# Short blocks merged ahead of the long sequence's last gate columns, output products by weight unit, late attention outputs split in place

## The chip, the cores and the metric

One core of one Trainium2 chip. The metric is the device time of the whole kernel in microseconds (us), as the median of several runs. Before the change it is 2817.07 us (three runs, 2802.38 to 2821.04).

## The reference

An encoder layer over two sequences (1 x 1024 and 1 x 2048 tokens, "short" and "long" here), with 16 meta tokens ahead of each, 1024 channels and shared weights. Cut to what matters:

```python
xn = rmsnorm(h, g_pre)
proj = xn @ w_in + b_in                        # 1024 -> 6672 columns
ya = (neighbourhood_attention(na_q, na_k, na_v, rpb) * silu(na_z)) @ w_a
yb = (mlstm(ml_qk, ml_v, ml_g, ml_o, ...) * silu(ml_z)) @ w_b
ga, gb = split(sigmoid(mg))                    # two gate vectors of 1024
y = (ga * ya + gb * yb) @ w_out
return h + rmsnorm(y, g_post)                  # the meta tokens are dropped
```

Attention has 8 heads of 64 over a window of 8 x 16 grid places; the mLSTM has 4 heads of 128 and runs in both directions in chunks.

## The kernel before

All products are made in fp32r with operands split in a rounded high and a low part, three matmuls each (high by high, low by high, high by low; lines 170 to 172 for the helper mm3). PE's instructions stand in the order in which the program writes them; those of the other engines are ordered by a scheduler at build time, each engine then taking its own in that fixed order. DMAs of these stages are issued from SP's queue, in order.

Two streams of work are interleaved on PE. The *dense* stream is written out in PLAN (line 44): projection columns per half sequence ("akqzt", "Gh" and so on: a = mLSTM q and k, k, q, z = attention, t = values and others token by token, G and h = gate columns), the first column groups of the short sequence by a seven-product scheme ("S"), and the items ("f", s, b), one for each block of 512 tokens: two for the short sequence (s = 0), four for the long one (s = 1). The *sparse* stream is the mLSTM and the attention of both sequences (STEPS, line 45): mLSTM short, attention short, mLSTM long, attention long; after each of its steps dense work of a set cost is put in. Dense work is what fills PE while the sparse steps wait for ACT and DVE.

An f item (final, line 1802) has two parts. The *merges*: for each of 8 channel tiles ft, four k steps of the mLSTM output (br = 1) and four of the attention output (br = 0) against w_b and w_a, each result times its gate (L1841), added (L1843), split in mh (ACT, L1844) and mlo (DVE, L1845). The inputs yh and yl of a block are loaded by yload (line 1763): it loads a finished output from DRAM into yl (L1774), rounds it into yh on ACT (L1793 is where the profile puts it) and subtracts on DVE (L1778). The attention's last step (na_out, line 1246) adds the two halves of a head (L1259, L1261), multiplies by the gate z (L1263) and writes the block's output to DRAM (L1264). The *output products* against w_out: four column blocks cq of 256 columns, each of two weight units (a = 0, 1: 512 input channels each), times four token tiles tt of 128. For a column block, both units are taken; each token tile has 8 k steps of three matmuls (L1875 to L1877) into a PSUM tile of its own, of three ("pj"); then ACT squares it into a sum (sqj, L1905) and DVE multiplies by g_post into yo (L1906). final_out normalises and adds the residual xres (L1956), and writes out (L1957). The last item makes column blocks 2 and 3 together, tile by tile, and closes each tile as soon as it is complete.

Weights come in units of 512 KB (wpump): the first time raw, rounded on ACT (L269), its low part on DVE (L270), and both stored (L285); later both parts are loaded (L262). Four buffers each (NBW) hold whi and wlo; a unit's buffer is given back by wdone, which starts the next load. g_post is held whole in one tile ("gain"), scaled once by -0.125 (L1859).

Of the kernel before, what the change touches and what calls it, by code (L numbers as in the profile page):

```python
# [18 lines left out]
P = 128  # L19
# [24 lines left out]
PLAN = ((0, 0, "akt"),) + FIRST + ((1, 0, "at"), (1, 1024, "akqzt"), (1, 0, "kqzGh"), (1, 1024, "Gh"), ("f", 0, 0), ("f", 0, 1), ("f", 1, 0), ("f", 1, 1), ("f", 1, 2), ("f", 1, 3))  # L44
# [81 lines left out]
class K:  # L126
# [3 lines left out]
    def __init__(self, tc, ins, outs):  # L130
        self.tc, self.nc = tc, tc.nc
        self.xs = []
        self.i, self.o = ins, outs
        self.wreq, self.wraw, self.wrdy, self.wout = deque(), deque(), deque(), 0
        self.wseen, self.wkept, self.xkept = set(), {}, {}
        self.rwait = {}
        self.xput, self.turn, self.last, self.turns = deque(), 0, None, False
        self.need, self.gpost = False, None
# [53 lines left out]
    def gain(self, name):  # L192

        g = self.wp.tile([P, D], F32, name="gain", bufs=1)
        self.nc.sync.dma_start(g, _bc(self.i[name], 0, D))
        return g
# [1049 lines left out]
    def na_out(self, np_, unit, s):  # L1246
# [15 lines left out]
        if hh and cb == 3:  # L1262
            nc.vector.tensor_tensor(yg, yg, zt, op=ALU.mult)  # L1263
            nc.sync.dma_start(self.YA[s][rt][pr][:, :], yg)  # L1264
# [294 lines left out]
    def ml_outputs(self, mp, s, h, g, NB, sts, norms):  # L1559
# [23 lines left out]
        def split(b):  # L1583
            if b < NB:
                raw = raws.pop(b)
                if s and b % 3 == 2 and self.gpost is None:
# [176 lines left out]
    def yload(self, s, b):  # L1763
# [17 lines left out]
        late, half = [4, 5, 6, 7, 0, 1, 2, 3], None  # L1781
        while todo or late or half is not None:
# [19 lines left out]
    def final(self, s, b, nxt):  # L1802
# [21 lines left out]
        for ft, br in [(0, 1)] + [x for f in range(KT) for x in ((f + 1, 1), (f, 0)) if x[0] < KT]:  # L1824
# [3 lines left out]
            for k in range(4 * br, 4 * br + 4):  # L1828
                self.need = True
                while k not in self.yk:  # L1830
                    if next(self.ygen) == "wait" and k not in self.yk:
                        yield True
# [24 lines left out]
        if self.fresh:  # L1857
            self.fresh = False
            nc.vector.tensor_scalar(self.gpost, self.gpost, -0.125, None, op0=ALU.mult)  # L1859
# [10 lines left out]
        def prods(p, tt, ws, k0, k1):  # L1870
            o = p[:, :256]
            xs = slice(tt * P, tt * P + P)
            for k in range(k0, k1):
                wh, wl = ws[k // 4][0][:, k % 4, :], ws[k // 4][1][:, k % 4, :]
                nc.tensor.matmul(o, mh[:, k, xs], wh, start=k == 0, stop=False)  # L1875
                nc.tensor.matmul(o, mh[:, k, xs], wl, start=False, stop=False)  # L1876
                nc.tensor.matmul(o, ml[:, k, xs], wh, start=False, stop=k == KT - 1)  # L1877

        for cqs in (((0,), (1,), (2,), (3,)) if nxt else ((0,), (1,), (2, 3))):
            wq = [self.wtake(2) for _ in cqs]  # L1880
            first = {}
            if cqs[0] == 0:
                for tt in range(2):
                    first[tt] = self.psum("pj", [P, 512])
                    prods(first[tt], tt, wq[0], 0, 7)
                    yield 21 * C256
            turns = [(tt, x) for tt in range(4) for x in zip(cqs, wq)]
            if len(cqs) > 1:
                turns[1:3] = turns[2], turns[1]
            for tt, (cq, ws) in turns:  # L1890
                if tt in first:
                    p = first[tt]
                    prods(p, tt, ws, 7, 8)
                else:
                    p = self.psum("pj", [P, 512])
                    prods(p, tt, ws, 0, 4)
                    if tt == 3:
                        self.wdone()
                    yield 12 * C256
                    prods(p, tt, ws, 4, 8)  # L1900
                if tt == 3:
                    self.wdone()
                o = p[:, :256]
                dst = yt[tt][:, cq * 256:(cq + 1) * 256]
                nc.scalar.activation(sqj, o, AF.Square, accum_out=ssq[:, tt, cq:cq + 1])  # L1905
                nc.vector.tensor_tensor(dst, o, self.gpost[:, cq * 256:(cq + 1) * 256], op=ALU.mult)  # L1906
                if cq == 3 and not nxt:
                    for _ in self.final_out(s, t0, yt, ssq, tt, tt + 1):
                        pass
                if nxt and hook is None:  # L1910
                    if nxt[0] != "f":
                        nres = []
                        hook = self.build_half(*nxt[:2], nres)
                    else:
                        hook = self.ystart(*nxt[1:])
                if hook:
                    next(hook, None)
                yield (3 if tt in first else 12) * C256
# [10 lines left out]
    def final_out(self, s, t0, yt, ssq, a, b):  # L1929
# [17 lines left out]
        r = self.rsqrt8(fp, sv[:, a:b], [P, b - a])  # L1947
        yield
# [14 lines left out]
    def dense(self, ctx):  # L1963
# [11 lines left out]
        for j, item in enumerate(PLAN):  # L1975
# [6 lines left out]
            if s == "f":  # L1982
                if self.gpost is None:
                    self.gpost = self.gain("g_post")
                    self.fresh = True
# [111 lines left out]
```

## Time and profile before

| | |
|---|---|
| three runs, median (lowest, highest) | 2817.07 us (2802.38, 2821.04) |
| the profiled execution, its own time | 2810.6 us |
| its span | 2808.8 us |
| mean granted TensorE clock | 0.989 |
| PE busy | 2728.9 us (97%) |
| DVE, ACT busy | 1729.2 us (62%), 1501.9 us (53%) |
| DMA | 666.47 MB, 237 GB/s |

"Busy" is the time in which an engine has an instruction running; matmuls are pipelined, so two neighbours overlap, and a matmul of 256 columns lasts 0.28 us in the rows but follows the one before it after 0.12. In rows of time, the columns are the start in us, the duration in us, the engine, the line, the operation, what is written and read, the shapes, and in brackets how long the engine stood idle before and who ended that. PEld is the load of the stationary operand. SPq is an issue of a DMA. In rows of stretches there are the busy time of each engine with its instructions, the granted TensorE clock (1.00 is full), the mean busy share of the 16 DMA engines, and GB/s.

From 1470 to 2060 us the mLSTM of the long sequence runs beside projection columns; from 2060 to 2690 its attention beside the first five f items; then the last item stands alone.

### The profile page before, as it was taken

How to read it: one execution, taken by the hardware profiler on the slowest of the kernel's cores; microseconds unless marked ns; L12 is line 12 of the kernel's file. 1: busy time of each engine (PE TensorE's matmuls, PEld its weight loads, DVE VectorE, ACT ScalarE, POOL GpSimd, SP SyncE). 2: the span in 40 equal slices, each digit the busy share in tenths (PEclk: the TensorE clock that was granted, in tenths of full speed). 3: DMA queues.
4: the chain of work that ended last, by engine and by line, in shares of the span. 5: the costliest groups of instructions: out<-in, count | busy, mean ns of one | idle time of the engine just before them, and what ended most of it. 6: DMA issues, size and time to landing. Idle time of an engine off the chain costs nothing.

```text
span 2808.8 us, 47866 instructions
## 1 busy us (share of the span) xinstructions
PE 2728.9 (97%) x16840; PEld 2427.4 (86%) x16840; DVE 1729.2 (62%) x4339; ACT 1501.9 (53%) x3348; POOL 124.4 (4%) x298
## 2 busy tenths in 40 slices
PE   8999999999999999999999999999999999999988
PEld 7899988879998778999977888888888898988978
DVE  5534664534667636566624767665667868787754
ACT  5222454433446646655534666565657676777731
POOL 0220000005000000320000000000000000000000
PEclk9999999999999999999999999999999999999989
DMA  9876753396656976756586566885599989898964
GB/s 370 327 252 216 241 181 105 104 349 203 189 171 200 328 232 203 224 178 212 189 286 208 196 208 203 275 280 172 171 314 327 292 268 302 247 323 281 275 216 174
DMA packets 354676, 666.47 MB, mean 237 GB/s; under 512 B 53796, under 2 KB 159220, under 8 KB 354436
## 3 DMA queue, kind: packets, MB, share of 16 engines
q1 hardware_dynamic: 347172, 654.37, 70.4%
q0 software_dynamic: 7264, 9.04, 1.2%
q8 instruction: 133, 2.18, 0.3%
q14 instruction: 107, 0.88, 0.1%
HBM read 446.24 MB, written 216.97 MB: 236 GB/s over the span
## 4 chain that ended last, share of the span: by engine, by line
PE 75%; DMA 14%; DVE 6%; ACT 3%; issue 1%; SPq 1%; DVEq 0%; ACTq 0%; POOLq 0%; POOL 0%
PE pj L170 11%; PE pj L171 11%; PE pj L172 11%; PE pj L619 6%; PE pj L621 6%; PE pj L620 6%; PE pj L1876 3%; PE pj L1875 3%; PE pj L1877 3%; PE sm L1254 2%; PE sm L172 2%; PE tr L1240 2%; PE sm L171 2%; PE sm L170 2%; DMA qk<-cpl 1%; DMA wlo<-wl 1%
## 5 line engine op out<-in xcount | busy, mean ns | idle before, releaser
L170 PE MATMUL pj<-xh,whi 128*128 128x512 f32 (+1 forms) x1480 | 581.7, 393 | 9.8 <-ACT st L544 7.8
L171 PE MATMUL pj<-xl,whi 128*128 128x512 f32 (+1 forms) x1480 | 567.9, 384 | 0.1
L172 PE MATMUL pj<-xh,wlo 128*128 128x512 f32 (+1 forms) x1480 | 566.6, 383 | 0.3 <-DVE wlo L270 0.3
L619 PE MATMUL pj<-whi,xh 128*128 128x256 f32 (+1 forms) x1536 | 438.8, 286 | 2.1 <-DVE stT L634 2.1
L620 PE MATMUL pj<-wlo,xh 128*128 128x256 f32 (+1 forms) x1536 | 432.5, 282 | 0.0
L621 PE MATMUL pj<-whi,xl 128*128 128x256 f32 (+1 forms) x1536 | 432.4, 282 | 0.0
L170 PEld LDWEIGHTS pj<-xh,whi 128*128 128x128 f32 x1480 | 280.2, 189 | 60.5 <-ACT st L544 8.6
L172 PEld LDWEIGHTS pj<-xh,wlo 128*128 128x128 f32 x1480 | 279.8, 189 | 58.0 <-DVE wlo L270 0.5
L171 PEld LDWEIGHTS pj<-xl,whi 128*128 128x128 f32 x1480 | 280.4, 189 | 46.5 <-issue 0.5
L619 PEld LDWEIGHTS pj<-whi,xh 128*128 128x128 f32 x1536 | 289.6, 189 | 2.7 <-DVE stT L634 2.3
L620 PEld LDWEIGHTS pj<-wlo,xh 128*128 128x128 f32 x1536 | 289.4, 188 | 0.2
L621 PEld LDWEIGHTS pj<-whi,xl 128*128 128x128 f32 x1536 | 289.3, 188 | 0.0
L1875 PE MATMUL pj<-whi,mh 128*128 128x256 f32 x768 | 222.1, 289 | 6.5 <-ACT whi L269 3.7
L1876 PE MATMUL pj<-wlo,mh 128*128 128x256 f32 x768 | 218.9, 285 | 3.8 <-DMA wlo<-wl 2.1
L1877 PE MATMUL pj<-whi,mlo 128*128 128x256 f32 x768 | 218.4, 284 | 0.0
L170 PE MATMUL pj<-yh,whi 128*128 128x512 f32 x384 | 156.6, 408 | 9.7 <-ACT yh L1793 9.7
L1875 PEld LDWEIGHTS pj<-whi,mh 128*128 128x128 f32 x768 | 147.5, 192 | 8.3 <-ACT whi L269 4.1
L171 PE MATMUL pj<-yl,whi 128*128 128x512 f32 x384 | 153.2, 399 | 1.3 <-DVE yl L1778 1.3
L172 PE MATMUL pj<-yh,wlo 128*128 128x512 f32 x384 | 152.7, 398 | 0.0
L1876 PEld LDWEIGHTS pj<-wlo,mh 128*128 128x128 f32 x768 | 147.5, 192 | 5.7 <-DMA wlo<-wl 2.6
L1877 PEld LDWEIGHTS pj<-whi,mlo 128*128 128x128 f32 x768 | 147.4, 192 | 0.0
L1243 DVE TENSOR_TENSOR pts<-tr,pts 96x384 fp32r<-96x384 f32 (+2 forms) x192 | 118.6, 618 | 46.7 <-ACT pts L1242 45.8
(378 smaller groups left out, 5643.8 us busy)
## 6 DMA issues: line engine op xcount, KB each, us to landing
whi<-wh SPq DMA_DIRECT2D x152, 512.0 KB
wlo<-wl SPq DMA_DIRECT2D x152, 512.0 KB
wraw<-wu SPq DMA_DIRECT2D x64, 512.0 KB
wh<-whi SPq DMA_DIRECT2D x64, 512.0 KB
wl<-wlo SPq DMA_DIRECT2D x64, 512.0 KB
gt<-st SPq DMA_DIRECT2D x96, 256.0 KB
tg<-gt SPq DMA_DIRECT2D x96, 256.0 KB
xt<-xt SPq DMA_DIRECT2D x32, 512.0 KB
```

Source lines behind the costliest of these rows:

```text
L170: mm(out, ah, bh, start=start, stop=False, **more)
L171: mm(out, ah, bl, start=False, stop=False, **more)
L172: mm(out, al, bh, start=False, stop=stop, **more)
L619: nc.tensor.matmul(o, xh, wh, start=k == 0, stop=False)
L620: nc.tensor.matmul(o, xh, wl, start=False, stop=False)
L621: nc.tensor.matmul(o, xl, wh, start=False, stop=k == KT - 1)
L1240: nc.tensor.transpose(pt[:ks, ch, :], pr_[:, ch * ks:(ch + 1) * ks], self.ident)
L1243: nc.vector.tensor_tensor(pts[:ks, :nb, 1, :], pt[:ks, :nb], pts[:ks, :nb, 0, :].bitcast(F32), op=ALU.subtract)
L1254: nc.tensor.matmul(av[:, cb % 2], vt[:ks, kc // 8 + ch].rearrange("p a b -> p (a b)"), pts[:ks, ch].rearrange("p a b -> p (a b)"), start=c ...
L1875: nc.tensor.matmul(o, mh[:, k, xs], wh, start=k == 0, stop=False)
L1876: nc.tensor.matmul(o, mh[:, k, xs], wl, start=False, stop=False)
L1877: nc.tensor.matmul(o, ml[:, k, xs], wh, start=False, stop=k == KT - 1)
```

## The change

- PLAN: the two items of the short sequence go ahead of (1, 1024, "Gh"), the gate columns of the long sequence's second half. The short merges so run beside the last mLSTM heads, and those gate columns beside attention.
- Output products: a weight unit is taken, used for all four token tiles, and given back, before the next is taken. The four half-done sums of a column block stand in two PSUM tiles, two token tiles in each. The last item's column blocks 2 and 3 keep a PSUM tile for each sum, in another order of tiles.
- g_post is loaded by column block into two small tiles (gp); the factor -0.125 moves to the row factors r (one small DVE operation more in each final_out). The mLSTM's third split buffer, which used the big tile until then, stays in use.
- na_out: when the merges' loader of that block has already begun and has not loaded this output, ACT and DVE split yg straight into yh and yl, without DRAM. This is so for 5 of the 24 outputs.
- The last item's merges take the third mLSTM product ahead of the first attention product.

```diff
-PLAN = (..., (1, 0, "kqzGh"), (1, 1024, "Gh"), ("f", 0, 0), ("f", 0, 1), ("f", 1, 0), ...)
+PLAN = (..., (1, 0, "kqzGh"), ("f", 0, 0), ("f", 0, 1), (1, 1024, "Gh"), ("f", 1, 0), ...)
...
-            nc.sync.dma_start(self.YA[s][rt][pr][:, :], yg)
+            if self.y and self.y[0] == (s, rt) and pr in self.ylate:
+                _, yh, yl = self.y
+                nc.scalar.activation(yh[:, pr], yg, AF.Copy)
+                nc.vector.tensor_tensor(yl[:, pr], yg, yh[:, pr].bitcast(F32), op=ALU.subtract)
+                self.ylate.remove(pr)
+                self.yk.add(pr)
+            else:
+                nc.sync.dma_start(self.YA[s][rt][pr][:, :], yg)
...
+        if not nxt:
+            order[2:4] = order[3], order[2]
...
+        def prods(o, tt, w, a, fresh):
             xs = slice(tt * P, tt * P + P)
+            for k in range(4):
+                f, q = 4 * a + k, w[0][:, k, :]
+                nc.tensor.matmul(o, mh[:, f, xs], q, start=fresh and f == 0, stop=False, skip_group_check=True)
+                nc.tensor.matmul(o, mh[:, f, xs], w[1][:, k, :], start=False, stop=False, skip_group_check=True)
+                nc.tensor.matmul(o, ml[:, f, xs], q, start=False, stop=f == KT - 1, skip_group_check=True)
+
+        def leave(o, tt, cq, gp):
+            nc.scalar.activation(sqj, o, AF.Square, accum_out=ssq[:, tt, cq:cq + 1])
+            nc.vector.tensor_tensor(yt[tt][:, cq * 256:(cq + 1) * 256], o, gp, op=ALU.mult)
+
+        gps = [self.gain(0), self.gain(1)]
+        for cq in range(4 if nxt else 2):
+            banks = [self.psum("pj", [P, 2, 256]) for _ in range(2)]
+            for a in range(2):
+                w = self.wtake(1)[0]
+                for tt in range(4):
+                    o = banks[tt // 2][:, tt % 2]
+                    prods(o, tt, w, a, tt % 2 == 0)
+                    if tt == 3:
+                        self.wdone()
+                    if a:
+                        leave(o, tt, cq, gps[cq])
...
+                    yield 12 * C256
+            if cq < 2:
+                gps.append(self.gain(cq + 2))
+        if not nxt:
+            ws = [[self.wtake(1)[0] for _ in range(2)] for _ in range(2)]
+            turns = [(0, 2), (1, 2)] + [x for tt in range(2, 4) for x in ((tt - 2, 3), (tt, 2))] + [(2, 3), (3, 3)]
+            for tt, cq in turns:
+                o = self.psum("pj", [P, 512])[:, :256]
...
+        nc.vector.tensor_scalar(r, r, -0.125, None, op0=ALU.mult)
```

How the instructions stand, at three places. First PE in the output products of the long sequence's third block, third column block, between two token tiles; the names in brackets are the engines that the row waits for (PE, DVE, Activation = ACT). Before:

```order
L1875 MATMUL pj<-whi,mh 128x256
L1876 MATMUL pj<-wlo,mh 128x256
L1877 MATMUL pj<-whi,mlo 128x256
L1240 MATMUL tr<-ident,prb 104x128 [waits PE_49]
L1240 MATMUL tr<-ident,prb 104x128 x2
L1254 MATMUL sm<-pts,vt 128x256 [waits DVE_49,Activation_49]
L1254 MATMUL sm<-pts,vt 128x256 x3
L1875 MATMUL pj<-whi,mh 128x256
L1876 MATMUL pj<-wlo,mh 128x256
L1877 MATMUL pj<-whi,mlo 128x256
```

And now, between the first and the second token tile of the second weight unit (the new lines 1882 to 1884 are the old 1875 to 1877):

```order
L1882 MATMUL pj<-whi,mh 128x256
L1883 MATMUL pj<-wlo,mh 128x256
L1884 MATMUL pj<-whi,mlo 128x256
L1254 MATMUL sm<-pts,vt 128x256 [waits DVE_49]
L1254 MATMUL sm<-pts,vt 128x256 x2
L1215 MATMUL sm<-kd,stk 128x312
L1216 MATMUL sm<-kx_24012,qB_24010 128x312
L1882 MATMUL pj<-whi,mh 128x256 [waits DVE_49]
L1883 MATMUL pj<-wlo,mh 128x256
L1884 MATMUL pj<-whi,mlo 128x256
```

The first matmul of the next token tile waits for DVE now; by the count of the semaphore, for the gain product (new line 1888) of the tile just done, which reads the other half of the same PSUM tile. The same stands at the fourth token tile, in each column block of each item but the last item's column blocks 2 and 3, 44 times in all.

Second, PE at the same step of a late mLSTM head of the long sequence (sc<-qkx are its scores). Before, projection columns stand around it:

```order
L170 MATMUL pj<-xh,whi 128x512
L171 MATMUL pj<-xl,whi 128x512
L172 MATMUL pj<-xh,wlo 128x512
L1637 MATMUL sc<-qkx 128x256
L1639 MATMUL sc<-qkx 128x128
L1637 MATMUL sc<-qkx 128x256
L1639 MATMUL sc<-qkx 128x128
```

Now merges of the short sequence (yh, yl):

```order
L170 MATMUL pj<-yh,whi 128x512
L171 MATMUL pj<-yl,whi 128x512
L172 MATMUL pj<-yh,wlo 128x512
L1644 MATMUL sc<-qkx 128x256
L1646 MATMUL sc<-qkx 128x128
L1644 MATMUL sc<-qkx 128x256
L1646 MATMUL sc<-qkx 128x128
```

All matmuls of the two short items have moved there, and the 768 of the gate columns to the first third of the long attention; the order from the long sequence's first item on is as it was, apart from the edits within the items.

Third, DVE at the end of the last attention head, beside the last item's first merges. Before:

```order
L1956 SCALAR_TENSOR_TENSOR yo<-yo,nwy,xres 128x512 x2
L1261 TENSOR_TENSOR yg<-sm,yg 64x2x8x16 x2
L1263 TENSOR_TENSOR yg<-yg,zt 128x512
L1956 SCALAR_TENSOR_TENSOR yo<-yo,nwy,xres 128x512 x2
L1778 TENSOR_TENSOR yl<-yl,yh 128x512
```

Now:

```order
L1966 SCALAR_TENSOR_TENSOR yo<-yo,nwy,xres 128x512 x2
L1261 TENSOR_TENSOR yg<-sm,yg 64x2x8x16 x2
L1263 TENSOR_TENSOR yg<-yg,zt 128x512
L1966 SCALAR_TENSOR_TENSOR yo<-yo,nwy,xres 128x512 x2
L1267 TENSOR_TENSOR yl<-yg,yh 128x512
```

The low half is taken straight from yg, at the same place in DVE's order: behind two residual additions of the item before.

More of the change, by code (lines that the diff above doesn't have):

```diff
@@ L1781, in yload @@
         late, half = [4, 5, 6, 7, 0, 1, 2, 3], None
+        self.ylate = late
         while todo or late or half is not None:
@@ L1830, in final @@
                 while k not in self.yk:
-                    if next(self.ygen) == "wait" and k not in self.yk:
+                    if next(self.ygen, "wait") == "wait" and k not in self.yk:
                         yield True
@@ new lines, in final @@
+                    if hook:
+                        next(hook, None)
+                    yield 12 * C256
+            if cq < 2:
[5 more added lines that the diff above has]
+                o = self.psum("pj", [P, 512])[:, :256]
+                for a in range(2):
+                    prods(o, tt, ws[cq - 2][a], a, True)
+                    if a == 0:
+                        yield 12 * C256
+                leave(o, tt, cq, gps[cq])
+                if cq == 3:
@@ L1908, in final @@
                     for _ in self.final_out(s, t0, yt, ssq, tt, tt + 1):
                         pass
[L1910 to L1918, printed above, removed]
+                yield 12 * C256
```

63 lines of the change are left out of this document (16 added, 47 removed).

## The prediction

> **What bounds the kernel now.** I read the page first, then the busy time by stage, then who PE waited for, then the two places that the change rewrites.
>
> ```profile
> span 2808.8 us, 47866 instructions
> PE 2728.9 (97%) x16840; PEld 2427.4 (86%) x16840; DVE 1729.2 (62%) x4339; ACT 1501.9 (53%) x3348; POOL 124.4 (4%) x298
> ```
>
> PE is the bound: DVE is next with 62%. The change adds and removes no matmul, so its gain can only come out of the idle 79.9 us (2808.8 - 2728.9) and out of stretches at a low clock, and any new PE wait is paid in full. The stages with the merges ("f" items) start at 2060; in the next rows each item is a merge stretch followed by an output-product stretch.
>
> ```profile
> core 0: us, PE busy (x) PEld busy (x) DVE busy (x) ACT busy (x) POOL busy (x), PEclk, DMA share, GB/s
> 1470.00:2060.00 590.00, 580.42 (x2999) 486.95 (x3000) 374.87 (x1214) 354.35 (x930) 3.89 (x23) 0.99 0.66 216
> 2060.00:2110.00 50.00, 49.71 (x232) 40.91 (x232) 36.93 (x65) 26.41 (x47) 0.00 (x0) 1.00 1.00 327
> 2110.00:2182.00 72.00, 66.06 (x506) 64.96 (x506) 50.35 (x113) 54.79 (x129) 0.00 (x0) 0.93 0.90 310
> 2242.00:2312.00 70.00, 66.09 (x514) 64.40 (x513) 46.52 (x109) 51.19 (x120) 0.00 (x0) 0.95 0.84 260
> 2312.00:2377.00 65.00, 62.24 (x313) 51.83 (x313) 57.70 (x131) 44.13 (x89) 0.00 (x0) 0.97 0.96 304
> 2629.00:2690.00 61.00, 61.00 (x507) 60.92 (x506) 42.63 (x105) 45.01 (x114) 0.00 (x0) 1.00 0.68 213
> 2690.00:2754.00 64.00, 51.91 (x217) 41.76 (x215) 32.41 (x62) 8.95 (x17) 0.00 (x0) 0.87 0.72 251
> 2754.00:2801.00 47.00, 46.38 (x386) 45.88 (x385) 18.03 (x64) 8.22 (x33) 0.00 (x0) 1.00 0.43 159
> ```
>
> Three stretches lose: the output products of the two short blocks (2110:2182, 2242:2312), and the last merges (2690:2754). The output products of the later items lose nothing (2629:2690 is 61.00 busy of 61.00). Who PE waited for from 2060 on:
>
> ```profile
> PE pj L170 <- ACT yh L1793: 9.7, 1, 9.7
> PE sm L1254 <- ACT prb L1223: 5.7, 4, 2.8
> PE pj L1875 <- ACT whi L269: 3.7, 2, 2.0
> PE pj L1875 <- DMA whi<-wh: 2.8, 1, 2.8
> PE sm L1254 <- DVE pts L1243: 2.4, 1, 2.4
> PE pj L1876 <- DMA wlo<-wl: 2.1, 2, 1.1
> PE pj L1876 <- DVE wlo L270: 1.7, 2, 0.9
> PE pj L171 <- DVE yl L1778: 1.3, 1, 1.3
> ```
>
> So weights that come late cost 3.7 + 2.8 + 2.1 + 1.7 = 10.3 us, and the last attention output 9.7. No row has PE waiting for the evacuation of an output product.
>
> **Gain 1, weights by unit.** Before, a column block takes two weight units at once and gives the buffers back at its end; now each is used by four token tiles in a row and given back after 48 matmuls, so a loaded unit lies ready three units ahead instead of two. The two short-block rows lose 72 - 66.06 = 5.9 and 70 - 66.09 = 3.9 us of idle time, and by their clocks (0.93 and 0.95) about 5.0 and 3.5 more: 18 together. Not all of it goes: the first item still fetches, rounds and stores its weights at a DMA share of 1.00 (2060:2110), now beside the mLSTM heads, whose stretch (1470:2060) has 0.66 already. I take **-15**, with -6 (the DMA still late) and -18 as ends.
>
> **Gain 2, the last attention output.** Before, it goes to DRAM and back:
>
> ```profile
> 2702.94 1.42 DVE L1956 SCALAR_TENSOR_TENSOR yo<-yo,nwy,xres 128x512 f32<-128x512 f32 x2 [2.03 <-DMA xres<-x_sample]
> 2705.29 0.69 DVE L1263 TENSOR_TENSOR yg<-yg,zt 128x512 f32<-128x512 f32 x1
> 2705.90 1.41 DVE L1956 SCALAR_TENSOR_TENSOR yo<-yo,nwy,xres 128x512 f32<-128x512 f32 x2
> 2706.01 0.36 SPq L1264 DMA_DIRECT2D ya<-yg  x1
> 2710.45 0.33 SPq L1774 DMA_DIRECT2D yl<-ya  x1
> 2713.72 0.63 ACT L1793 ACTIVATE yh<-yl 128x512 fp32r<-128x512 f32 x1 [11.78 <-DMA yl<-ya]
> 2714.40 0.80 PE L170 MATMUL pj<-yh,whi 128*128 128x512 f32 x1 [9.68 <-ACT yh L1793]
> ```
>
> From the end of the product with the gate (2705.98) to the rounding (2713.72) are 7.7 us, all of it DMA. Now ACT can round at 2706.0 and end at 2706.6. But DVE's row of the low half stands behind two residual additions (third place in the order rows), which run to 2707.3; with 0.69 of its own it is ready at 2708.0. PE stands there from 2703.8 on, since four triples (3 matmuls of 0.23 each, 2.8 us) follow the last weighted sum, which began at about 2700.5 and takes 0.5. So 9.7 becomes some 4: -5.7. Of the product that is moved ahead, two triples stand before the last transposes and one between these and the last weighted sum (2.1 us), in which DVE works off its queue, so the 2.4 us wait for pts becomes 0.5: -1.9. The half clock that follows both (0.87 over 64 us is 8.3, part of it in the idle time itself) gives back another 3. In all **-10.5**, ends -5 and -14. Four other outputs, of the sample's third and last blocks, are split in place as well; with the 1.3 us wait for yl above I take **-2** (+4 to -6: their split now stands in ACT's and DVE's queues among the attention work, while five writes and five loads leave SP's queue).
>
> **Loss 1, a new wait in the output products.** Four token tiles now share two PSUM tiles, two halves each. The first order rows show what follows: in the second half-sum the second and the fourth tile's first matmul wait for DVE, and the wait is for the gain product of the tile just before it, which reads the other half of the same PSUM tile. Before, each tile had a PSUM tile of its own out of three, and PE went on. This stands in every column block that goes by unit: 5 items x 4 blocks x 2 and 1 x 2 x 2, **44 waits**. What one costs is read from an evacuation of before, from the tile's last matmul to the end of its gain product:
>
> ```profile
> 2774.16 0.28 PE L1877 MATMUL pj<-whi,mlo 128*128 128x256 f32 x1
> 2774.55 0.38 ACT L1905 ACTIVATE sqj<-pj 128x256 bf16<-128x256 f32 x1 [2.38 <-PE pj L1877]
> 2774.83 0.20 ACT L1905 ACTIVATION_READ_ACCUMULATOR sqj<-pj 128x1 f32 x1
> 2775.05 0.42 DVE L1906 TENSOR_TENSOR yo<-pj,gain 128x256 f32<-128x256 f32 x1 [2.43 <-ACT sqj L1905]
> ...
> 2147.21 0.28 PE L1877 MATMUL pj<-whi,mlo 128*128 128x256 f32 x1
> 2148.17 0.37 ACT L1905 ACTIVATE sqj<-pj 128x256 bf16<-128x256 f32 x1
> 2149.45 0.42 DVE L1906 TENSOR_TENSOR yo<-pj,gain 128x256 f32<-128x256 f32 x1
> ...
> L1906 DVE TENSOR_TENSOR yo<-pj,gain 128x256 f32<-128x256 f32 x96 | 40.3, 421 | 47.2 <-ACT sqj L1905 46.4
> ```
>
> With idle engines that is 2775.47 - 2774.16 = 1.31 us; behind other work on ACT and DVE it is 2.66 (2149.87 - 2147.21). The same subtraction over all 96 gives a mean of 1.53. PE could have gone on one matmul pitch (0.12) after the last one's start, and takes some 0.05 to wake: 1.53 - 0.12 + 0.05 = 1.46 us per wait, 64 us for 44. What PE has in between hides a part: the attention or mLSTM matmuls that stand between the two tiles. Counted in the order rows and priced by pitch (0.12 for 256 columns, 0.23 for 512, 0.09 a transpose) they are 19 us in all, with nothing at all between in 12 of the 44, the four of the last item among them. So **+45**, with 44 x (1.31 - 0.07) - 19 = 36 as the low end and 60 as the high end, half way towards the slow evacuation. Behind the waiting matmul stand all other matmuls, attention's too, so ACT and DVE are fed later as well; they have room (DVE is busy 43 to 58 us of 61 to 72 in the rows above).
>
> [...]
>
> **Loss 2, the clock.** One wait of 2.76 us halved the clock behind it, one of 1.30 did not:
>
> ```profile
> 2339.08 1.01 PE L1254 MATMUL sm<-pts,vt 128*128 128x256 f32 x3 [2.76 <-ACT prb L1223]
> 2338.60:2342.00 3.40, 2.92 (x8) 2.46 (x9) 3.25 (x7) 1.65 (x5) 0.00 (x0) 0.50 1.05 272
> 2578.08 0.50 PE L171 MATMUL pj<-yl,whi 128*128 128x512 f32 x1 [1.30 <-DVE yl L1778]
> 2576.00:2579.40 3.40, 2.10 (x11) 1.44 (x10) 2.90 (x7) 1.55 (x5) 0.00 (x0) 1.00 1.04 378
> ```
>
> A halved stretch of 3.4 us costs 1.7. Most new waits are near 1.3, so I take two or three such stretches, **+4**; none, and twelve (+20, the share of slow evacuations), are the ends.
>
> [...]
>
> **The rest.** The gain vector comes in 24 transfers of 128 KB in place of one; each is asked for a column block ahead, so its cover is the 11 us of a block, and its refill holds SP only until the gain product of the block's fourth tile, about one evacuation: 0, up to +3. The moved order (short merges beside the mLSTM heads, the last gate columns beside attention) is 0 by itself, -6 to +5: PE's 9.6 us of idle time in 590 there show little to win. The short items bring all their transfers along; beside attention their stages moved 260 to 327 GB/s, and mLSTM with columns 216 at a share of 0.66, so the DMA gets near full there and has room beside the gate columns, which fetch less. At the very end the third tile's closing work now starts one tile later:
>
> ```profile
> 2799.88 1.42 DVE L1956 SCALAR_TENSOR_TENSOR yo<-yo,nwy,xres 128x512 f32<-128x512 f32 x2
> 2801.21 0.42 DVE L1906 TENSOR_TENSOR yo<-pj,gain 128x256 f32<-128x256 f32 x1
> ```
>
> Before, its two additions (1.42) were through when the last gain product came; now they and some single-column steps stand behind that product and ahead of the last tile's own, with one more scaling step: **+2**, ends 0.5 and 3.
>
> **Sum.** -15 - 10.5 - 2 + 45 + 4 + 2 = +23.5 us. The profiled execution took 2810.6 (span 2808.8), 6.5 under the median of the three runs; the mean of all four is 2812.8. I put the sum on that mean: **2836 us**, 0.7% above the median. A measurement of this kernel tells about 1% (28 us) from no change, so the forecast is slower, but inside what counts as the same.
>
> **The rivals.**
> *The waits are swallowed* (not slower). While PE stands at a half-filled tile, ACT, DVE and the DMA work ahead, and the stalls that are left in these stages (prb 5.7, pts 2.4, the weights) vanish in it. For it: the waits and the stalls lie in the same stretches. Against it: the new waits stand even in stretches that lose nothing now (2629:2690). With the low ends, 36 + 0 + 0.5, and gains of 18 + 14 + 6, the sum is -1.5; if the waits also overlap with the 8 us of prb and pts, about -10: **2803**. It decides once a wait costs less than 21.5 / 44 = 0.49 us on average (the 21.5 are all other terms together).
> *The waits stretch* (clearly slower). ACT and DVE take their instructions in a fixed order, and an evacuation may stand behind attention or mLSTM work as in the 2.66 us case. For it: the first item now rounds its weights beside mLSTM heads, on both engines, with DMA near its limit. Against it: most evacuations of before took 1.25 to 1.6. With 60 for the waits and 12 for the clock: 2836 + 15 + 8 + 4 for the rest = **2863**.
> *The in-place split does not pay*: if DVE's residual additions wait for their transfer, the low half comes as late as now, and gain 2 is 0 instead of 10.5: **2847**. For it: in the trace those additions stood 2.0 us at their transfer just before.
>
> **How the numbers follow.** Forecast (2818 to 2850) 0.55; swallowed 0.20; stretched 0.15; no gain from the split 0.10. The range for 8 in 10 goes from 2806, just above "swallowed", to 2864, which takes "stretched" in. Slower by over 1% (above 2845): all of "stretched", half of "no gain from the split" and a quarter of the forecast, 0.35. Faster by over 1% (under 2789): the far end of "swallowed", 0.06. The same: 0.59.
>
> **What would show it.** In the profile after: PE waits put down to the gain product (yo, the new line 1888), some 40 of them, about 1 us each, where before there is none; the output-product stretches at 90% busy, the last item's with four waits of 1.2 us and no cover; no more whi or wlo waits there; the wait before the last merges at 3 to 4 us instead of 9.7. The forecast is wrong if the yo waits sum to under 25 us, or if the stages from the first merge on are not longer than now.

## The result and the profile after

The changed kernel takes 2850.9 us (median of four runs, 2845.01 to 2854.64), the kernel before 2815.65 us beside it: a ratio of 1.0135, with a 95% interval from 1.0099 to 1.017. That is 35 us slower, where 23.5 were predicted; it lies inside the predicted range (2806 to 2864), 1 us above the forecast's own interval (2818 to 2850), and on the other side of the 1% bound (slower, to which the prediction gave 0.35; the interval begins at 0.99%). The profiled execution took 2852.78 us.

The head of its page:

```profile
span 2851.0 us, 47874 instructions
PE 2738.2 (96%) x16840; PEld 2427.9 (85%) x16840; DVE 1729.2 (61%) x4347; ACT 1505.4 (53%) x3348; POOL 123.7 (4%) x298
```

The work is the same; PE's idle time grew from 79.9 to 112.8 us (2851.0 - 2738.2), and its busy time by 9.3 us (2738.2 - 2728.9). Who PE waited for, from 1380 us on (total, times, longest, in us), without the smaller rows:

```profile
PE pj L1882 <- DVE yo L1888: 37.0, 40, 3.3
PE tr L1765 <- DVE den L1688: 6.0, 1, 6.0
PE tr L1765 <- DVE mv L1750: 4.3, 1, 4.3
...
PE pj L170 <- ACT yh L1266: 2.0, 1, 2.0
...
PE pj L171 <- DVE yl L1267: 0.8, 1, 0.8
```

The first row is the predicted new wait, 40 times. The rows for weights (whi, wlo) in the output products are gone, and the last attention output now costs 2.0 + 0.8 instead of 9.7 + 1.3 us. The second and third rows were not foreseen: they are the transposes of the mLSTM's norm output, which stand in the short merges' new place. (Of the names in these rows, num, den, mv and hb belong to the mLSTM's output and its norm; prb, further down, are attention's weights, and pts their transposed high and low parts.) By stage, in the columns known from the prediction:

```profile
1833.00:1898.00 65.00, 60.60 (x328) 51.53 (x327) 62.65 (x161) 44.02 (x103) 0.00 (x0) 1.00 0.95 340
1898.00:1981.00 83.00, 64.43 (x495) 61.92 (x495) 54.03 (x179) 46.01 (x138) 0.00 (x0) 0.94 0.72 246
1981.00:2041.00 60.00, 57.81 (x291) 48.52 (x291) 54.52 (x138) 29.26 (x78) 0.00 (x0) 0.97 0.87 316
2041.00:2111.00 70.00, 60.98 (x493) 59.73 (x493) 43.04 (x161) 34.98 (x105) 2.46 (x8) 0.98 0.78 258
2111.00:2340.00 229.00, 229.00 (x1168) 191.83 (x1167) 122.35 (x299) 150.96 (x307) 1.02 (x2) 1.00 0.69 219
2401.00:2472.00 71.00, 64.19 (x508) 61.34 (x507) 46.42 (x107) 48.98 (x116) 0.00 (x0) 1.00 0.75 232
2739.00:2790.00 51.00, 48.22 (x211) 38.85 (x210) 31.85 (x61) 7.35 (x13) 0.00 (x0) 0.97 0.83 289
2790.00:2841.00 51.00, 46.73 (x384) 45.82 (x383) 16.85 (x59) 7.76 (x31) 0.00 (x0) 1.00 0.42 151
```

The first four rows are the two short items beside mLSTM: merges, products, merges, products. They lose 278 - 243.8 = 34.2 us of PE time, most of all in the first products (83.00, of which 18.6 idle). The gate columns beside attention (fifth row) lose nothing. The long items' products are busy 90% (64.19 of 71.00), where before they were full. The last merges (2739 to 2790) take 51 us instead of 64. The first row shows DVE busy 62.65 us of 65.00; in the row 2060:2110 of before it was 36.93 of 50.00.

PE's matmuls that waited in the last item's output products, where nothing stands between two token tiles:

```profile
2797.38 0.28 PE L1884 MATMUL pj<-whi,mlo 128*128 128x256 f32 x1
2798.68 0.39 PE L1882 MATMUL pj<-whi,mh 128*128 128x256 f32 x1 [1.02 <-DVE yo L1888]
2798.91 0.28 PE L1883 MATMUL pj<-wlo,mh 128*128 128x256 f32 x1
...
2817.04 0.39 PE L1882 MATMUL pj<-whi,mh 128*128 128x256 f32 x1 [1.08 <-DVE yo L1888]
```

There are four, as the order rows said, here the first and the last, at 1.0 to 1.1 us (1.2 was forecast). The idle time is not the whole price. From the start of the last matmul before the wait to the first behind it are 1.30 us, and to the next one 0.23, where each follows after 0.12 in full flow: 1.29 us lost with 1.02 idle. Counted like this, from start to start, the 40 waits cost 47.8 us, 1.2 each. The difference to 37.0 stands in the rows as busy time, which fits most of the 9.3 us above.

The longest of all stands in the first short item; DVE's and PE's rows there:

```profile
1918.98 0.69 DVE L1760 TENSOR_TENSOR hb<-hb,szg 128x512 f32<-128x512 f32 x1 [3.60 <-DMA szg<-sz]
1919.59 0.42 DVE L1888 TENSOR_TENSOR yo<-pj,gp 128x256 f32<-128x256 f32 x1
...
1920.06 0.58 PE L1882 MATMUL pj<-whi,mh 128*128 128x256 f32 x1 [3.35 <-DVE yo L1888]
```

The gain product stood in DVE's queue behind a product with the mLSTM's gate (szg) whose transfer was late; PE paid 3.35 us for it.

### The profile page after: what moved, and what is told of

Read it like the earlier page. It is cut to its first block, busy times and chain, and to the rows that moved or that the text cites. A ratio compares the mean times of both kernels' runs of the same rounds, so it can differ in the third digit from the quotient of the medians.

```text
span 2851.0 us, 47874 instructions
## 1 busy us (share of the span) xinstructions
PE 2738.2 (96%) x16840; PEld 2427.9 (85%) x16840; DVE 1729.2 (61%) x4347; ACT 1505.4 (53%) x3348; POOL 123.7 (4%) x298
## 4 chain that ended last, share of the span: by engine, by line
PE 77%; DMA 11%; DVE 6%; ACT 3%; issue 1%; SPq 1%; DVEq 0%; ACTq 0%; POOL 0%; POOLq 0%
PE pj L170 12%; PE pj L171 12%; PE pj L172 12%; PE pj L619 6%; PE pj L620 6%; PE pj L621 6%; PE pj L1882 3%; PE pj L1884 3%; PE pj L1883 3%; PE sm L1254 2%; PE tr L1240 2%; PE sm L172 2%; PE sm L171 2%; PE sm L170 2%; DMA qk<-cpl 1%
```

## The experiments

Each kernel was run in five rounds beside the kernel before; the ratios are to that, and 0.1% is 2.8 us. In the expectations "the prompt" is the short sequence and "the sample" the long one. The first four part the change into its pieces. Theory A is the prediction's: the two token tiles in one PSUM tile. Theory B, formed from the profile after, is the moved order; C is that the new waits only cover old ones.

**e1_alt.** Neighbouring token tiles in different PSUM tiles, all else as changed:

```diff
-                    o = banks[tt // 2][:, tt % 2]
-                    prods(o, tt, w, a, tt % 2 == 0)
+                    o = banks[tt % 2][:, tt // 2]
+                    prods(o, tt, w, a, tt < 2)
```

> The changed kernel, but neighbouring token tiles of an output-product block lie in different PSUM tiles (first and third share one, second and fourth the other), so that between an evacuation and the next write to its PSUM tile stands one whole token tile, 12 matmuls or about 1.4 us. Nothing else is changed. Theory A (the loss is the wait for the other half's evacuation, and it is paid in full): PE's waits for the gain product fall from 37.0 us to under 10, and the time from 2851 to about 2822 (2815 to 2828). Theory B (the loss is the moved order, short merges beside the mLSTM heads): the waits for yo go, but the stretches between 1833 and 2111 us lose nearly as much to other waits, and the time stays above 2840. Theory C (the waits only hide other stalls): yo falls under 10 and the waits for weights, prb and pts come back by 15 us or more; the time is 2830 to 2840.

Measured: 2804.62 us, 0.9971 (0.996 to 0.9983), 46 us below the changed kernel. PE's waits in the same view, and three stretches (the first short merges, a long item's products, the last item's products):

```profile
PE tr L1765 <- DVE den L1688: 6.0, 1, 6.0
PE tr L1765 <- DVE mv L1750: 4.3, 1, 4.3
...
PE pj L1882 <- DVE yo L1888: 1.8, 1, 1.8
```

```profile
1828.00:1893.40 65.40, 62.24 (x330) 52.76 (x329) 62.94 (x162) 44.27 (x104) 0.00 (x0) 0.97 0.97 339
...
2380.00:2442.00 62.00, 62.00 (x507) 61.32 (x507) 44.99 (x106) 47.43 (x113) 0.00 (x0) 1.00 0.85 265
2747.00:2793.00 46.00, 46.00 (x386) 45.76 (x384) 17.08 (x61) 7.75 (x31) 0.00 (x0) 1.00 0.45 164
```

The products are full again, with the same two PSUM tiles and the same waits in the program: only the 12 matmuls (1.4 us) that now stand between an evacuation and the next write of its PSUM tile are new. A's mechanism holds and C falls. The gain is beyond A's own range (2815 to 2828), and 9 to 11 us more than the idle time that went (37.0 - 1.8 = 35.2). Counted from start to start, the waits that went are about 46 us (47.8 - 2.1), and that is the gain. The clock has no part in it: behind the first merge nine stretches of 3.4 us stand at half clock in e1 and eight in the changed kernel. The rows of the mLSTM transposes did not move by a tenth, so they are not a consequence of the new wait.

**e2_oldplan** and **e3_alt_oldplan.** The old PLAN line in the changed kernel, and in e1_alt:

```diff
-..., (1, 0, "kqzGh"), ("f", 0, 0), ("f", 0, 1), (1, 1024, "Gh"), ("f", 1, 0), ...
+..., (1, 0, "kqzGh"), (1, 1024, "Gh"), ("f", 0, 0), ("f", 0, 1), ("f", 1, 0), ...
```

> The changed kernel with the old plan: the sample's last gate columns stand ahead of the prompt's two merge items again, as in the kernel before. The products by weight unit and the split in place stay. Theory A (the shared PSUM tiles cost the loss): 44 waits for yo stay, 35 to 40 us, and the time stays at 2851 within 8. Theory B (the moved order costs about 12 us of it: the two short items lost 46 us between 1833 and 2111, and the gate columns beside attention lost none): the transposes of the mLSTM norm output no longer wait (6.0, 4.3, 1.9 and 1.8 us now), and the time falls to 2839 or lower. If the moved order is what made the weights come in time, weight waits of 5 to 10 us return and the time rises above 2855.

> Both of the former: neighbouring token tiles in different PSUM tiles, and the old plan. Theory A: within 6 us of the run that only parts the PSUM tiles, about 2822. Theory B: the two gains add up, 2805 to 2812, below the kernel before (2815.65). Theory C: no lower than 2825.

Measured: e2 2838.86 us, 1.009 (1.0077 to 1.0102), 12 below the changed kernel; e3 2795.92 us, 0.9934 (0.992 to 0.9948), 8.7 below e1 and 9 under the end of B's own range (2805 to 2812). In e2 the predicted wait stands in almost all of its 44 places:

```profile
PE pj L1882 <- DVE yo L1888: 41.4, 43, 2.4
```

So both theories hold, each for its own share. The shared PSUM tiles cost 43 to 46 us (e2 against e3, changed against e1), the moved order 9 to 12 (changed against e2, where the intervals just meet; e1 against e3, where they do not). They add up. The expected return of weight waits with the old order stayed small: 3.2 us (whi 1.7, wlo 1.5) in e3 and 0.8 in e2.

**e4_before_end** and **e10_split_only.** The kernel before with the end of the change alone: the split in place and the product moved ahead; and with the split only.

```diff
+            if self.y and self.y[0] == (s, rt) and pr in self.ylate:
+                _, yh, yl = self.y
+                nc.scalar.activation(yh[:, pr], yg, AF.Copy)
+                nc.vector.tensor_tensor(yl[:, pr], yg, yh[:, pr].bitcast(F32), op=ALU.subtract)
...
+        if not nxt:                                  # e4 only
+            order[2:4] = order[3], order[2]
```

> The kernel before with the end alone of the change: attention's last outputs split in place, and the third product of the last merges ahead of the second; old plan, old output products. By the prediction's gain 2 (10.5 + 2 us, the changed kernel's last stretches gained 15.7 us) the wait before the last merges falls from 9.7 to 3 to 4 us and the time from 2815.65 to about 2803 (2798 to 2808). Rival: the gain came from the products by unit in the neighbouring stretches, and the end alone gives under 4 us, 2812 or more.

> The kernel before with the split of attention's last outputs in place alone; the order of the last merges stays as before. It parts gain 2. By the prediction the split by itself takes the 9.7 us wait to about 4 and brings 5.7 us, the order of the products brings 1.9 more and the clock 3: so 2809 - 7 = about 2802 here, against about 2793 with both. Rival (the split is all of it): within 3 us of the run with both, 0.9933 of the kernel before. Rival (the split does not pay without the order): within 3 us of the kernel before.

Measured: e4 2795.24 us, 0.9933 (0.992 to 0.9945): 16 to 19 us faster than before, more than the 12.5 of the prediction (gain 2 and the other splits) and than the expectation. e10 2796.32 us, 0.9954 (0.9942 to 0.9967), where about 2802 was expected. PE's waits in the last merges, of e4 and then of e10:

```profile
PE pj L170 <- ACT yh L1266: 2.0, 1, 2.0
PE pj L171 <- DVE yl L1267: 0.8, 1, 0.8
```

```profile
PE pj L170 <- ACT yh L1266: 3.2, 1, 3.2
PE sm L1254 <- DVE pts L1243: 1.8, 1, 1.8
PE pj L171 <- DVE yl L1267: 0.8, 1, 0.8
```

That stretch lasts 63.8 us before, 56.0 in e10 and 51.4 in e4. The split is 7.8 of it, the order of the products 4.6; the pts wait of the prediction (2.4) is still there without the order and gone with it. By the times alone, the two kernels can hardly be told apart.

**e5_unit_only.** e3 with the old end: products by unit alone, with neighbouring tiles in different PSUM tiles.

```diff
-            order[2:4] = order[3], order[2]
+            pass
...
-            if self.y and self.y[0] == (s, rt) and pr in self.ylate:
...
+            nc.sync.dma_start(self.YA[s][rt][pr][:, :], yg)
```

> Products by weight unit alone: old plan, neighbouring token tiles in different PSUM tiles (so without the new wait), and the end as in the kernel before (last attention outputs through DRAM, old order of the last merges). It isolates gain 1 (-15 predicted; ends -6 and -18). If the unit order is worth that by itself, the time is 2811 - 12 = about 2799 (2795 to 2804). With the end added (the run of both, 2795.92) it had brought nothing over the end alone (2795.24); if that is so here too, 2811 within 4: the weight waits go, and other waits take their place in the merges beside attention (4.1, 6.3 and 7.1 us lost there in the run with both, 1.5, 4.9 and 0.6 in that with the end alone).

Measured: 2805.48 us, 0.9982 (0.997 to 0.9995), between the two expectations: -1 to -8 us, not -12. In its own place the unit order does what it should. The two short items' products in e5:

```profile
2120.00:2187.50 67.50, 63.27 (x507) 62.36 (x507) 51.11 (x115) 54.23 (x128) 0.00 (x0) 0.97 1.02 348
2248.00:2311.60 63.60, 63.09 (x511) 61.78 (x510) 45.94 (x106) 49.98 (x119) 0.00 (x0) 1.00 0.96 287
```

They take 131 us instead of 142 (2110:2182 and 2242:2312 of before). But with the end of the change added, the unit order brought nothing that the times show: e3 and e4 differ by 0.7 us, and their intervals leave room for 5 us either way. In e3 the merges of the first three long items, beside attention, take 197.8 us (2303.4 to 2367.9, 2430.4 to 2497.1, 2559.3 to 2625.9), in e4 187.6. So the 8.7 us won in the short products (132.9 in e3, 141.6 in e4) are given back there in these two profiles. PE's waits from the first to the last of these merges, e3 and then e4:

```profile
PE sm L1254 <- ACT prb L1223: 5.4, 2, 3.2
PE sm L1254 <- DVE pts L1243: 4.2, 1, 4.2
```

```profile
PE sm L1254 <- ACT prb L1223: 4.5, 3, 3.1
```

That is 5.4 us of waits more in e3, counted with a small row that is not shown. The rest fits the clock: e3's three merges spent 13.7 us at half clock, e4's 3.4, which is 5.1 us of time. The size of the loss is not firm, though: the same merges take 192.3 us in e7 below, which differs from e3 only by a buffer of the mLSTM, 192.6 in e5 and 191.0 in the kernel before.

**e8_mix** and **e12_mix_pool.** e4 with the unit order (tiles in different PSUM tiles) in the short sequence's two items alone; and the same with the merges' addition on GpSimd:

```diff
+        for cq in range(0 if s else 4):      # by unit, as in e1_alt
...
-        for cqs in (((0,), (1,), (2,), (3,)) if nxt else ((0,), (1,), (2, 3))):
+        for cqs in () if s == 0 else (((0,), (1,), (2,), (3,)) if nxt else ((0,), (1,), (2, 3))):
...
-                nc.vector.tensor_tensor(ms[0], ms[0], ms[1], op=ALU.add)
+                nc.gpsimd.tensor_tensor(ms[0], ms[0], ms[1], op=ALU.add)      # e12 only
```

> The kernel before with the end of the change, and the unit order (neighbouring tiles in different PSUM tiles) in the two prompt items alone, where the weights were late; the sample's four items keep the column order, which lost nothing there. If the unit order in the sample's items is what cost the 10 us in their merges, the gain in the prompt's output products (13.1 + 4.8 us lost with columns, 7.8 + 1.5 by unit) is kept and the time is 2786 (2783 to 2790). If the attention beside the merges simply loses what the output products win, whatever the order there, 2795 within 3.

> The run with the unit order in the prompt's items alone (2786.22), and every merge's addition of its two halves (0.68 us on DVE, 48 of them) on GpSimd. The sample's merges beside attention lost 4.3, 6.7 and 0.6 us there to waits for prb and pts. If DVE's load is behind these, they shrink and the time falls by 5 or more, to 2781 or lower; if they come from ACT and the fixed order, it stays within 3 us of 2786; if GpSimd's addition is too slow for the next product, the last merges (with no attention beside them) lose 3 us or more and the time rises.

Measured: e8 2786.22 us, 0.992 (0.9901 to 0.9939); e12 2781.33 us, 0.9904 (0.9889 to 0.9919), the fastest of all: 27 us under the kernel before, 65 to 70 under the changed one. PE's waits in the three merges beside attention and the products between them, e8 and then e12:

```profile
PE sm L1254 <- ACT prb L1223: 6.3, 3, 3.5
PE sm L1254 <- DVE pts L1243: 0.8, 1, 0.8
```

```profile
PE sm L1254 <- ACT prb L1223: 2.5, 2, 2.1
PE sm L1254 <- DVE yg L1261: 1.4, 1, 1.4
```

e8's median is 9 us below e4's, as if the gain in the short products (131.1 us in e8) were kept; but by the ratios it is 4 us, with intervals that overlap, so this is not shown. Its merges beside attention take 192.0 us, between e4's 187.6 and e3's 197.8, although their items have the column order again. That speaks against the unit order in the long items as the cause of the longer merges, but it is one profile, of an execution of 2794.55 us, 8 above e8's median. In e12 these merges take 185.0 us. The step from e8 to e12 (4.9 us of the medians) has overlapping intervals, and the 7.0 us in the merges compare that profile with one at e12's median: what the addition on GpSimd is worth here is not shown.

**e6_alt_tz** and **e7_alt_oldplan_tz.** Why does the moved order cost 10 us? The first idea was the late szg. A third buffer for the mLSTM's gates, in e1_alt and as a control in e3:

```diff
-                tzs[b // 2] = [mp.tile([P, 4, P], F32, name=n, tag="tz", bufs=2) for n in ("tog", "szg")]
+                tzs[b // 2] = [mp.tile([P, 4, P], F32, name=n, tag="tz", bufs=3) for n in ("tog", "szg")]
```

> The run with parted PSUM tiles and the new plan, with one buffer more for the mLSTM output gates (three instead of two), so that the load of szg no longer waits until DVE has used the szg before. Theory: the moved order costs 9 to 12 us because in the short merges DVE stands 4.6 us at a szg that was asked for only when the buffer came free (1909.99, used at 1915.10), and the transposes behind it wait 6.0 and 4.3 us. Then both waits fall under 2 us and the time from 2804.6 to about 2797 (2794 to 2800). Rival: the lateness is DVE's or the DMA's load in general, and the time stays within 3 us of 2804.6.

> Control for the former: the same third buffer with the old plan, where szg came in time beside the gate columns. Theory: no gain there, 2796 within 3. If the third buffer helps by itself (the stage from 870 to 1155 us loses 14 to 21 us in all runs, with the same loads), 2790 or lower.

Measured: e6 2801.55 us, 0.997 (0.9959 to 0.9982), no different from e1's 0.9971; e7 2791.38 us, 0.9933 (0.9916 to 0.9949), by the ratio no different from e3's 0.9934. Between 1820 and 2100 us PE's waits in e6 are still

```profile
PE tr L1765 <- DVE den L1688: 6.0, 1, 6.0
PE tr L1765 <- DVE mv L1750: 4.3, 1, 4.3
```

and DVE's own wait in e1, which e6 has no more:

```profile
DVE hb L1760 <- DMA szg<-sz: 5.8, 2, 4.6
```

The idea fell: the late szg is real, but in these kernels the time does not show it. e6 against e7 is a third measurement of the moved order, 10 us.

**e9_norm_later** and **e11_add_pool.** Two further tries from e6: the transposes four steps later, and the short merges' additions on GpSimd.

```diff
-        for _ in range(10):
+        for _ in range(14 if s else 10):             # e9
...
-                nc.vector.tensor_tensor(ms[0], ms[0], ms[1], op=ALU.add)
+                (nc.vector if s else nc.gpsimd).tensor_tensor(ms[0], ms[0], ms[1], op=ALU.add)      # e11
```

> The run with the third gate buffer (new plan, parted PSUM tiles), and the transposes of the sample's mLSTM norm output four steps later in the order (14 steps after the norm instead of 10). The third buffer took DVE's 5.8 us at szg away, and PE's waits of 6.0 and 4.3 us stayed to the tenth; so szg was not their cause. Theory D (the norm's chain over DVE and ACT is a fixed number of PE steps long, and too long for them where the merges come between): both waits go, and the time falls from 2801.55 by 6 to 10, to about 2793. Theory E (DVE is full in the short merges, 63.37 us busy of 65.70, so that whatever stands behind it waits): the two rows go or shrink, other DVE waits of the same sum take their place, and the time stays within 4 us of 2801.55.

> The run with the third gate buffer, and the addition of the two halves of a merge (0.68 us on DVE, 16 of them) on GpSimd instead of DVE in the prompt's two items. Theory E (DVE is full in the short merges beside mLSTM: 63.37 us busy of 65.70 and 54.92 of 62.00): DVE's busy time falls by 5.5 us in each of these merge stretches, PE's waits for DVE there shrink, and the time falls from 2801.55 by 5 or more. Theory D (length of the norm's chain in the fixed order): the time stays within 3 us. If GpSimd is so slow at it that mh comes late, PE waits at the output products and the time rises.

Measured: e9 2807.19 us, 0.9994 (0.9984 to 1.0003), 6 slower than e6, outside both expectations; e11 2806.33 us, 0.9987 (0.9975 to 0.9998), 5 slower, with an interval that still meets e6's. In e9 the two rows are gone, and these stand in their place (1820 to 2095 us):

```profile
PE pj L1882 <- DVE yo L1888: 6.7, 4, 3.8
PE tr L170 <- ACT num L1674: 3.9, 3, 1.6
PE sm L170 <- DVE num L1679: 3.7, 3, 2.2
```

Theory D (a chain too long for its place) falls: room for that chain only moved the wait (all of PE's waits there sum to 20.3 us in e6 and 19.6 in e9). This is what E (DVE full) says of the rows, though not of the time, since the run got slower, and one of the new rows is ACT's. e11 can't speak for or against E, because it did not relieve DVE; the time rose as in its third case, but without that case's sign, for no row has PE waiting for mh. The first short merges of e6 and of e11, from their first matmul to the first products, then DVE's row for the weights' low part there in each:

```profile
1828.00:1893.70 65.70, 61.27 (x331) 52.03 (x331) 63.37 (x163) 44.07 (x104) 0.00 (x0) 1.00 0.97 341
```

```profile
1833.20:1905.60 72.40, 63.77 (x330) 54.22 (x329) 67.74 (x167) 46.40 (x111) 12.62 (x7) 0.95 0.88 303
```

```profile
L270 DVE TENSOR_TENSOR wlo<-wraw,whi 128x1024 fp32r<-128x1024 f32 x9 | 10.9, 1214 | 1.3 <-ACT whi L269 1.3
```

```profile
L270 DVE TENSOR_TENSOR wlo<-wraw,whi 128x1024 fp32r<-128x1024 f32 x9 | 14.6, 1622 | 0.5 <-ACT whi L269 0.4
```

With the additions on GpSimd these merges last 72.4 us instead of 65.4, for the same matmuls, and DVE is busy 67.74 us of them instead of 63.37 (in a stretch cut 0.3 us wider): some of its instructions took longer while GpSimd added, 1622 ns instead of 1214 on average here.

Where the moved order loses its time can be read from the pairs e1 and e3, e6 and e7. The PE work up to the long sequence's first merge is the same in each pair, only ordered otherwise. It is done at 2319.2 us in e1 and at 2303.4 in e3 (2319.6 and 2301.5 in e6 and e7); behind it the moved order wins 3 to 6 us back. From PE's 9000th matmul (about 1417 us) to that merge, PE's idle time put down to DVE is 19.4 us in e1 and 9.0 in e3 (20.0 and 7.3 in e6 and e7), that put down to ACT 6.5 and 7.7 (9.1 and 5.2), and 27.3 us instead of 13.7 run at half clock in both pairs. So the loss is waits for DVE, with the halved clock. Whether they come from DVE's queue, which is 96% busy in the first short merges, or from the order in which DVE gets its work, no run here parts; neither the late szg nor the place of the transposes is the cause.

## Why the prediction was right and where it was not

Step by step, from the kernel before to the changed one: the end of the change -0.67% (e4), products by unit with parted PSUM tiles 0.0% (e3 against e4; the longer tail of the last tile is in it), the moved order +0.37% (e1 against e3), two token tiles side by side in one PSUM tile +1.64% (changed against e1). That is -19, 0, +10 and +46 us. Against the prediction's terms, the unit order missed by 15 us and the moved order by 10 one way, the end by 6 and the clock by 4 the other way. The mechanism of the main term was right; that the total came out within 15 us of the forecast is in part luck.

- *Loss 1, the new wait: right*, in mechanism, place and size. 45 us were predicted (36 to 60), 43 to 46 measured by taking it away. The profile shows 40 waits, of 44 places in the program: 37.0 us of idle time, 0.93 each, and 47.8 us from start to start, the way in which the prediction had priced them (from the pitch of the matmul before). e1_alt shows that such a wait costs next to nothing (1.8 us, in one place) as soon as one tile's work lies between.
- *Gain 2 and the other splits: right in kind, too small.* 12.5 us were predicted and 16 to 19 measured. The wait fell to 2.8 us in all, where "some 4" was said, and the order of the last products brought 4.6 us in its stretch, where 1.9 and a share in the clock's 3 were said.
- *Gain 1, weights by unit: the mechanism right in its own stretch, the size at the end wrong.* The waits for weights fell from 10.3 us to none in the changed kernel's output products (3.2 in e3's), and the short products are 9 to 11 us shorter by themselves. But of the 15 us in the sum 1 to 8 arrive alone (e5) and, beside gain 2, none within 5 us (e3 against e4); these two do not differ clearly. The step that failed is that time won in one stretch was taken as won for the end. Longer merges beside attention, with waits for prb and pts and a halved clock, took it back in the profile of e3; why they are longer, and how much of that returns from run to run, stays open.
- *The moved order: the step that failed.* "0 by itself, -6 to +5" was worked out from PE's idle time and the DMA. DVE was not looked at: the short merges brought their additions, gate products and the low parts of weights beside mLSTM heads, DVE went to 62.65 us busy of 65.00, and the waits for it before the long sequence's first merge rose by 8 to 13 us. The moved order cost 9 to 12 us, beyond the end of its range. That DVE's load is behind it is likely, not shown.
- *Loss 2, the clock: too high.* +4 was put in for halved stretches behind the new waits. One of the 40 was followed by one, the one of 3.35 us; the other halved stretches behind 1833 us follow other rows' waits, single long ones (6.0, 4.3 and 3.2 us) or two close together (1.2 and 0.9, 2.0 and 0.8).
- *The tail: small, as predicted.* From PE's last matmul to the end are 9.4 us instead of 8.3; +2 was said.

Of the rivals, "the waits are swallowed" had its deciding point at 0.49 us per wait, and 0.93 came. "The waits stretch" gives a time that fits about as well as the forecast (2863), but not for its reason: the waits summed to about what was forecast, and what was missing came from the moved order and from gain 1. "The in-place split does not pay" gives the nearest time of all (2847), and its condition fell: the last merges waited 2.8 us, and e10 shows the split worth 7.8 us in its stretch. The forecast's own tests held: over 25 us of yo waits, and longer stages from the first merge on.

## What to carry to other kernels

When several accumulations share a PSUM tile, write the tiles in such an order that the neighbour in time is never the neighbour in the tile: the same two tiles cost 45 us one way and nothing the other. Price such a wait from start to start of the matmuls around it, not by the idle time alone. Before work is moved beside other work, add up every engine's busy time in the new stretch, not only the bound engine's idle time. And a stall that is taken away inside a stream of two interleaved chains can be worth less at the end than in its own stretch, so time it together with the rest of the change.

## What the runs showed of the hardware

**Behind 2.30 us of PE work in 3.40 the clock stayed full, behind 1.72 it was halved.** In the changed kernel's last merges the wait of 2.0 us begins in the first of these stretches of 3.4 us and ends in the second, and that of 0.8 us lies in the second:

```profile
2749.40:2752.80 3.40, 2.30 (x12) 1.60 (x10) 3.22 (x6) 0.38 (x1) 0.00 (x0) 1.00 1.03 401
2752.80:2756.20 3.40, 1.72 (x6) 1.22 (x7) 2.58 (x5) 0.63 (x1) 0.00 (x0) 1.00 0.99 339
2756.20:2759.60 3.40, 3.40 (x9) 2.65 (x9) 1.63 (x3) 0.63 (x1) 0.00 (x0) 0.50 0.82 253
```

The second row, behind 2.30 us of PE work, stands at clock 1.00, the third, behind 1.72, at 0.50. A wait of 1.1 us leaves 2.3 of 3.4 us, as in the first row, and one of the 40 new waits had a halved stretch behind it, the one of 3.35 us: PE was busy 0.21 us in the 3.40 ahead of that stretch. A bound between 2.30 and 1.72 is not shown.

**In e11 some of DVE's instructions took longer beside GpSimd's additions.** The 128x512 addition of e11 took 1604 ns on GpSimd (679 on DVE in e6), and in the first short merges DVE's subtraction for the weights' low part (L270) went from 1214 to 1622 ns on average, up to 2287, while its gate product (L1852) stayed at 678 and 677 ns. Five of the nine subtractions took 1226 ns or less. Why these and not the others, no run here shows.
